# A hybrid diffusion step on one core: adaLN chunks in other places, squares ahead of the scaled copies, a fourth unnormed tile behind the pool layer

## The chip, the cores and the metric

The kernel runs on one NeuronCore of a Trainium2 chip. The metric is the device time of one launch in microseconds (us). Five engines matter: TensorE (PE, matrix products), ScalarE (ACT, copies and activation functions), VectorE (DVE, elementwise work), the SyncE queue (SP), which issues the weight transfers, and the DMA engines. GpSimd does nearly nothing here.

## The reference, cut to what matters

One inference step of a trunk of four layers with D = 1024 channels over 384 tokens: 128 context tokens and 256 latent tokens, each group with a conditioning vector of its own. All weights are float32.

```python
for i in range(DEPTH):                                # 4 layers
    kind = i % 3                                      # 0 gMLP, 1 pool, 2 attention
    sh1, sc1, gt1, sh2, sc2, gt2 = split(silu(cond) @ w_ada[i] + b_ada[i], 6)
    h = rms_norm(x, g_mix[i]) * (1 + sc1) + sh1
    y = mixer[kind](h)
    x = x + gt1 * y
    h = rms_norm(x, g_ffn[i]) * (1 + sc2) + sh2
    a, u = split(h @ w_ffn_in[i], 2)                  # 2 x 2816 columns
    x = x + gt2 * ((gelu(conv3(a)) * u) @ w_ffn_out[i])
```

The line with `w_ada` is the adaLN: for each layer six vectors of 1024 values, for two conditionings, each from a 1024 x 1024 block of weights. That is 24 blocks of eight 128 x 1024 chunks.

## The kernel before

**Activations and products.** x lies transposed in SBUF, as eight tiles d of 128 channels x 384 tokens. A float32 product is made of three passes at reduced precision: a weight is split into `whi` (a rounded copy) and `wlo` (the rest), an activation into `hh` and `hl`, and `mm3` (L688) adds hh·whi, hh·wlo and hl·whi in PSUM.

**Weights.** All weights come in one long list of chunks, in the order of a plan (`chunk_plan`), each of 128 x 1024 float32 (512 KB), through a ring of five buffers `wraw`. The SP queue issues them in order, and a buffer is given back in order. ACT makes `whi` of a chunk (L349), DVE makes `wlo` (L356), up to three chunks ahead of PE, in four buffers each.

**The phases.** For each layer the plan has the mixer's phases (`gr`, `gv`, `gu`, `go` for gMLP; `p` for the pool layer; `qkv`, `at`, `o` for attention) and then the FFN's: `fr` and `fi` (the first product, 22 tiles f of 128 columns of a and of u) and `fo` (the second). Below, go0, fo0, fi1, o2 and so on name a phase and its layer; go3 is that of the last layer. An output phase (go, o, fo) works through the output tiles d in pairs (0,1), (2,3), (4,5), and then 6 and 7 alone.

**adaLN chunks.** They stand in the same list, between the weight chunks. The table `ADA` says which of them belong to which phase, and the planner (`weave`) spreads them over the phase. An "ad" chunk is worked on DVE: two multiply-and-sum instructions of 1024 elements (L391), one for each conditioning. An "ap" chunk is worked on PE (L409). Since all engines run their own instructions in program order, an ad chunk stands on DVE between the `wlo` of its neighbours.

**Residual and what follows it.** When an output tile d is done, `residual` (L464) adds it to x on DVE, in two instructions (context and latent tokens). Then `prep.after(d)` makes what the next sub-layer needs before the norm is known: ACT writes hh = round(A·x) in two instructions (L624), DVE writes hl = A·x - hh in two (L626), ACT squares x (L477) and DVE adds the square to `acc` (L479). At the end the sum's last term is added (L484), PE sums over partitions (`cs`, L536), and from that comes the factor `rbs` of the norm. In fo0 ACT also adds the pool's bias to x (L1655). In the pool layer the residual stands at L1057. The output phase fo1, ahead of attention, makes squares only, and fo3 nothing.

**Unnormed tiles.** The first product of an FFN begins before the norm is known: its first `NR` = 3 tiles f use A·x as it stands, and the factor `rbs` is applied to the results on DVE (L714, L719). Meanwhile `norm` makes normed activations for the later tiles (L585 to L598).

**The start.** In layer 0 the first adaLN block (`a0`) is needed at once: its chunks are multiplied on PE (L1550) between the products of gMLP's first phase (L862), through a `hook` that `vmm` calls after the first of the three products of each k.

Of the kernel before, what the change touches and what calls it, by code (L numbers as in the profile page):

```python
# [99 lines left out]
def chunk_plan():  # L100
# [11 lines left out]
    for l in range(DEPTH):  # L112
# [15 lines left out]
        if kind == 0:  # L128
            phase(l, "go", out_chunks("go", j, 16))
        elif kind == 2:  # L130
            phase(l, "at", [])
            phase(l, "o", out_chunks("o", j, 8))
            n = len(plan) - len(out_chunks("o", j, 8))
            plan[n - 6:n + 2] = plan[n:n + 2] + plan[n - 6:n]
        phase(l, "fi", [("fr", l, kk, 0) for kk in range(4)] + [("fi", l, f, kk) for f in range(2, NF)
# [145 lines left out]
class Prog:  # L281
# [326 lines left out]
    def prep(self, l, which, extra=None):  # L608


        nc = self.nc
        self.ada_need(l, 3 * which + 1)
        A = self.gains(l, which)
        sh = self.prm[:, l, 24 * which:24 * which + 8, :]
        res = {"acc": self.new_acc(), "A": A}

        def after(d):
            if d == 5:
                self.ada_need(l, 3 * which)
                nc.vector.tensor_copy(self.hh[:, :, T:TE], sh)  # L620
                nc.vector.tensor_tensor(out=self.hl[:, :, T:TE], in0=sh, in1=self.hh[:, :, T:TE].bitcast(F32),
                                        op=ALU.subtract)
            for c, (t0, t1) in enumerate(GRPS):
                nc.scalar.activation(self.hh[:, d, t0:t1], self.x[:, d, t0:t1], AF.Copy, scale=A[:, d, c:c + 1])  # L624
            for c, (t0, t1) in enumerate(GRPS):
                nc.vector.scalar_tensor_tensor(out=self.hl[:, d, t0:t1], in0=self.x[:, d, t0:t1],  # L626
                                               scalar=A[:, d, c:c + 1], in1=self.hh[:, d, t0:t1].bitcast(F32),
                                               op0=ALU.mult, op1=ALU.subtract)
            res["sq"] = self.square(d, res["acc"])
            if extra is not None:  # L630
                extra(d)

        return res, after
# [56 lines left out]

    def ffn(self, l, pr, follow, stat_k):

# [5 lines left out]
        with self.tc.tile_pool(name=f"ffn{l}", bufs=1) as fp:  # L698
# [11 lines left out]
            def epi_a(f, pa, pu):  # L710
                if f >= NR:
                    return f, pa, None, pu, None
# [9 lines left out]
            def epi_b(st):  # L722
# [4 lines left out]
                for c, (t0, t1) in enumerate(GRPS):  # L727
                    p0, p1 = pos[c]
                    if f < NR:
                        nc.scalar.activation(ab[:, p0:p1], a1[:, t0:t1], AF.Identity, bias=be[:, c:c + 1])  # L730
                    else:
                        nc.scalar.activation(ab[:, p0:p1], a1[:, t0:t1], AF.Copy)
# [7 lines left out]
            def epi_c(st, t):  # L740
                f, _, _, u, bu = st
                g = self.tmp.tile([128, T], F32, tag="gg", name="gg")
                if f >= NR:
                    for c, (t0, t1) in enumerate(GRPS):
# [46 lines left out]
            for f in range(2, NF):  # L791
                w0 = TE if f < NR else T
                pa, pu = self.bank()[:, :w0], self.bank()[:, :w0]
                now, prev = (prev, []) if f == 5 else (prev[:1], prev[1:])
                for kk in range(2):
# [4 lines left out]
                    else:  # L800
                        gs = [epi_c(st, t) for st, t in zip(sts, ts)]
                        w = self.w_get("fi")
                        for st, g in zip(sts, gs):
                            self.split_act(g, gh[st[0]], gl[st[0]])
                    if f < NR:
                        norm(3)
                    for k4 in range(4):
                        k = 4 * kk + k4
                        r = (hh[:, k, :], hl[:, k, :]) if f < NR else (nh[:, k, :], nl[:, k, :])
                        self.mm3([(pa, 256 * k4), (pu, 256 * k4 + 128)], w, r, k == 0, k == 7)  # L810
# [30 lines left out]
    def gmlp(self, l, j, prep, pr=None, hook=None):  # L841
# [7 lines left out]
        with self.tc.tile_pool(name=f"gmlp{l}", bufs=1) as gp:  # L849
# [7 lines left out]
            def vmm(ps, w, cs, k):  # L857
                for p in range(3):
                    for i in range(3):
                        for n, c in enumerate(cs):  # L860
                            hs = (vl if p == 2 else vh)[:, k, 128 * i:128 * i + 128]
                            nc.tensor.matmul(ps[n][i], hs, w[p == 1][:, c:c + 512],  # L862
                                             start=(k == 0 and p == 0), stop=(k == 7 and p == 2))
                    if p == 0 and hook is not None and len(cs) == 2:
                        hook(k)

# [635 lines left out]
    def run(self):  # L1502
# [104 lines left out]

        def hook(k):
            if k + 1 < KD:
                a0_put(k + 1, a0_fin(k + 1))  # L1610
                a0_mm(k + 2)
            if k == 3:
# [9 lines left out]
        for l in range(DEPTH):  # L1622
            kind, j = l % 3, l // 3
            prep = lambda l=l: self.prep(l, 1)
            if l == 0:
                pr = self.gmlp(l, j, prep, None, hook)
            elif kind == 0:
# [31 lines left out]

            pr = self.ffn(l, pr, follow, 4 if kind == 1 else 2)  # L1660
        self.mm_ctx.close()
# [38 lines left out]
```

## Time and profile before

| what | value |
|---|---|
| median of 3 runs | 1789.51 us (1787.81 to 1791.0) |
| the profiled execution, its own time | 1788.39 us |
| span of the profiled execution | 1786.6 us |
| PE busy | 1754.6 us, 98% |
| PE's weight loads busy | 1675.2 us, 94% |
| DVE busy | 1371.8 us, 77% |
| ACT busy | 872.2 us, 49% |
| chain that ended last | PE 61%, DVE 22%, ACT 8%, DMA 4% |

How to read it: the busy share is an average over stages of different kinds. Where the time of PE's gaps goes is to be read from the rows at each gap, which name the engine and the line that ended the wait. The granted clock (PEclk) is a share of 2.4 GHz; 0.5 is the lower level, 1.2 GHz.

### The profile page before, as it was taken

What the parts mean: (1) busy time and instruction counts of PE and PEld (TensorE: products, weight loads), DVE (VectorE), ACT (ScalarE), POOL (GpSimd) and SP (SyncE); (2) the same over time, 40 slices, a digit from 0 to 9 for tenths busy, and PEclk for the clock granted to TensorE, in tenths of its full rate; (3) what the DMA queues carried; (4) which work ended last, traced back from release to release, by engine and by line L of the source; (5) the groups of instructions that cost most, each with busy time, mean ns of one, the idle gap of its engine ahead of it and who ended that gap; (6) DMA issues with size and microseconds to landing.
All of it is one profiled execution on the core that took longest, in us unless ns stands there. A gap on an engine that the chain in (4) does not pass through costs nothing.

```text
span 1786.6 us, 26835 instructions
## 1 busy us (share of the span) xinstructions
PE 1754.6 (98%) x10230; PEld 1675.2 (94%) x10230; DVE 1371.8 (77%) x2369; ACT 872.2 (49%) x1635; POOL 1.8 (0%) x30
## 2 busy tenths in 40 slices
PE   9999989999999999999998999999999999999999
PEld 7799889999998899998777999999988999999999
DVE  5888688888986888899687788887775767876632
ACT  3644236545455654432469565453454434755521
POOL 0000000000000000000000000000000000000000
PEclk9999999999999999999999999999999999999999
DMA  8764663555663355567550335655546344354341
GB/s 323 280 222 147 234 211 130 189 191 198 219 212 106 126 181 200 200 214 241 203 183 1 131 130 188 197 176 202 193 150 204 112 145 145 123 175 151 136 150 57
DMA packets 87636, 311.64 MB, mean 174 GB/s; under 512 B 10450, under 2 KB 10962, under 8 KB 87252
## 3 DMA queue, kind: packets, MB, share of 16 engines
q1 hardware_dynamic: 87220, 309.92, 50.9%
q8 instruction: 80, 1.31, 0.3%
q14 instruction: 48, 0.39, 0.1%
q10 hardware_dynamic: 288, 0.01, 0.0%
HBM read 308.06 MB, written 1.84 MB: 173 GB/s over the span
## 4 chain that ended last, share of the span: by engine, by line
PE 61%; DVE 22%; ACT 8%; issue 5%; DMA 4%; SPq 0%; DVEq 0%; ACTq 0%
PE mm L688 45%; DVE wlo L356 7%; DVE junk L391 7%; PE mm L862 6%; DMA wraw<-wts 4%; ACT whi L349 3%; DVE ct L736 3%; PE S L688 1%; PE mm L906 1%; ACT gg L745 1%; DVE gl L606 1%; PE adaT L688 1%; PE S L1138 1%; PE adaT L862 1%; PE psa L862 1%
## 5 line engine op out<-in xcount | busy, mean ns | idle before, releaser
L688 PE MATMUL mm<-hb,whi 128*128 128x384 f32 (+1 forms) x4064 | 888.7, 338 | 6.6 <-ACT whi L349 2.6
L688 PEld LDWEIGHTS mm<-hb,whi 128*128 128x128 f32 x4064 | 722.7, 189 | 11.6 <-ACT whi L349 3.3
L356 DVE TENSOR_TENSOR wlo<-wraw,whi 128x1024 fp32r<-128x1024 f32 (+2 forms) x390 | 466.3, 1201 | 213.7 <-ACT whi L349 212.4
L349 ACT ACTIVATE whi<-wraw 128x1024 fp32r<-128x1024 f32 (+2 forms) x390 | 399.3, 1034 | 270.3 <-PE mm L688 139.4
L688 PE MATMUL mm<-hb,wlo 128*128 128x384 f32 (+1 forms) x2032 | 521.4, 337 | 0.8 <-DVE wlo L356 0.8
L391 DVE SCALAR_TENSOR_TENSOR junk<-wraw,condb 128x1024 bf16<-128x1024 f32 x304 | 371.6, 1222 | 9.1 <-ACT condb L1618 2.7
L688 PEld LDWEIGHTS mm<-hb,wlo 128*128 128x128 f32 x2032 | 369.1, 189 | 1.3 <-DVE wlo L356 1.3
L745 ACT ACTIVATE gg<-ct 128x128 f32<-128x128 f32 (+1 forms) x152 | 47.0, 357 | 248.9 <-DVE ct L736 248.9
L688 PE MATMUL mm<-gh,whi 128*128 128x384 f32 x448 | 123.9, 338 | 3.2 <-ACT whi L349 3.2
L688 PE MATMUL mm<-gh,wlo 128*128 128x384 f32 x448 | 124.2, 338 | 2.4 <-DVE wlo L356 2.4
L688 PE MATMUL mm<-gl,whi 128*128 128x384 f32 x448 | 123.8, 338 | 0.0
L736 DVE SCALAR_TENSOR_TENSOR ct<-ab,par,ct 128x385 f32<-128x385 f32 x176 | 108.7, 619 | 6.4 <-ACT ct L734 2.7
L624 ACT ACTIVATE hb<-x,A 128x128 fp32r<-128x128 f32 x96 | 43.2, 457 | 103.9 <-DVE x L464 93.1
L862 PE MATMUL mm<-whi,hb 128*128 128x512 f32 x320 | 87.6, 399 | 0.0
L688 PEld LDWEIGHTS mm<-gh,whi 128*128 128x128 f32 x448 | 81.9, 189 | 4.1 <-ACT whi L349 4.1
L688 PEld LDWEIGHTS mm<-gh,wlo 128*128 128x128 f32 x448 | 82.0, 189 | 3.6 <-DVE wlo L356 3.6
L688 PEld LDWEIGHTS mm<-gl,whi 128*128 128x128 f32 x448 | 82.3, 189 | 0.0
L746 DVE TENSOR_TENSOR gg<-mm,gg 128x384 f32<-128x384 f32 x76 | 42.4, 558 | 47.4 <-ACT gg L745 46.7
L862 PEld LDWEIGHTS mm<-whi,hb 128*128 128x128 f32 x320 | 60.8, 190 | 15.6 <-ACT hb L573 0.4
L734 ACT ACTIVATE ct<-ab,par 128x385 f32<-128x385 f32 x88 | 62.7, 713 | 3.4
L464 DVE SCALAR_TENSOR_TENSOR x<-mm,prm,x 128x128 f32<-128x128 f32 x92 | 33.6, 411 | 22.9 <-PE mm L688 22.7
L862 PE MATMUL mm<-wlo,hb 128*128 128x512 f32 x160 | 47.8, 405 | 0.0
(286 smaller groups left out, 1651.8 us busy)
## 6 DMA issues: line engine op xcount, KB each, us to landing
wraw<-wts SPq DMA_DIRECT2D x562, 512.0 KB, 3.9
wraw<-wts SPq DMA_DIRECT2D x12, 256.0 KB, 2.6
wraw<-wts SPq DMA_DIRECT2D x8, 384.0 KB, 4.1
x<-x SPq DMA_DIRECT2D x4, 384.0 KB, 4.5
mx<-mix SPq DMA_DIRECT2D x1, 1280.0 KB, 7.8
y<-x SPq DMA_DIRECT2D x3, 384.0 KB, 3.1
condb<-condb SPq DMA_DIRECT2D x1, 1024.0 KB, 7.1
ws<-a_w_s SPq DMA_DIRECT2D x2, 512.0 KB, 4.3
```

What stands on the lines that cost most here:

```text
L349: nc.scalar.activation(hi[:, :n], t[:, :n], AF.Copy)
L356: nc.vector.tensor_tensor(out=lo[:, :n], in0=t[:, :n], in1=hi[:, :n].bitcast(F32), op=ALU.subtract)
L391: nc.vector.scalar_tensor_tensor(out=self.junk.bitcast(BF16), in0=w, scalar=1.0, in1=self.condb[:, c, :], op0=ALU.mult, op1=ALU.mult, accu ...
L464: nc.vector.scalar_tensor_tensor(out=x[:, d, t0:t1], in0=ps[:, t0:t1], scalar=self.prm[:, l, ty * 8 + d, c:c + 1], in1=x[:, d, t0:t1], op0 ...
L606: nc.vector.tensor_tensor(out=lo, in0=src, in1=hi.bitcast(F32), op=ALU.subtract)
L624: nc.scalar.activation(self.hh[:, d, t0:t1], self.x[:, d, t0:t1], AF.Copy, scale=A[:, d, c:c + 1])
L688: nc.tensor.matmul(o, w[:, c:c + nw], r, start=(first and p == 0), stop=(last and p == 2))
L734: nc.scalar.activation(t, ab[:, 1:T + 2], AF.Identity, scale=cw[1], bias=cb)
L736: nc.vector.scalar_tensor_tensor(out=t, in0=ab[:, i:i + T + 1], scalar=cw[i], in1=t, op0=ALU.mult, op1=ALU.add)
L745: nc.scalar.activation(g[:, t0:t1], t[:, t0 + c:t1 + c], GELU)
L746: nc.vector.tensor_tensor(out=g, in0=u, in1=g, op=ALU.mult)
L862: nc.tensor.matmul(ps[n][i], hs, w[p == 1][:, c:c + 512], start=(k == 0 and p == 0), stop=(k == 7 and p == 2))
```

## The change

Four things are changed, and no result is computed differently otherwise than by the order of roundings.

1. `prep.after(d)`: the square (ACT) and its sum (DVE) stand first. Then ACT writes A·x in two instructions into a buffer `xt`, ACT copies it to hh in one instruction, and DVE makes hl = xt - hh in one plain subtraction instead of two scaled ones.
2. The table `ADA`: ad chunks per phase, before and after: gu0 10 and 12, go0 12 and 8, fi0 18 and 18, fo0 16 and 18, fi1 18 and 20, fo1 22 and 20, fi2 16 and 18, fo2 12 and 14, gv3 8 and 8, go3 4 and 8, fi3 8 and 8. The eight chunks of block (2, 5) were ap chunks in attention, and are now ad chunks in fi2; the phase "at" and the exchange of two `o` chunks with six of them are gone.
3. The FFN behind the pool layer takes `NR` + 1 = 4 unnormed tiles.
4. At the start the hook is in two: the finished adaLN values are put to use after the first product of a k, and the next `a0` products (L1550) stand after its second product (`wlo`) instead of after the first.

```diff
--- before.py
+++ after.py
@@ -46,19 +46,18 @@
-    (0, "gu"): [("ad", 0, 2), ("ad", 0, 3, 0, 2)],
-    (0, "go"): [("ad", 0, 3, 2, 8), ("ad", 0, 5, 0, 6), ("ap", 1, 1)],
-    (0, "fi"): [("ad", 0, 5, 6, 8), ("ad", 1, 2), ("ad", 1, 0)],
-    (0, "fo"): [("ad", 1, 4), ("ad", 1, 3)],
-    (1, "fi"): [("ad", 1, 5), ("ad", 2, 1), ("ad", 2, 0, 0, 2)],
-    (1, "fo"): [("ad", 2, 0, 2, 8), ("ad", 2, 4), ("ad", 2, 3)],
+    (0, "gu"): [("ad", 0, 2), ("ad", 0, 3, 0, 4)],
+    (0, "go"): [("ad", 0, 3, 4, 8), ("ad", 0, 5, 0, 4), ("ap", 1, 1)],
+    (0, "fi"): [("ad", 0, 5, 4, 8), ("ad", 1, 2), ("ad", 1, 0, 0, 6)],
+    (0, "fo"): [("ad", 1, 0, 6, 8), ("ad", 1, 4), ("ad", 1, 3)],
+    (1, "fi"): [("ad", 1, 5), ("ad", 2, 1), ("ad", 2, 0, 0, 4)],
+    (1, "fo"): [("ad", 2, 0, 4, 8), ("ad", 2, 4), ("ad", 2, 3)],
-    (2, "at"): [("ap", 2, 5)],
-    (2, "fi"): [("ad", 3, 1), ("ad", 3, 2)],
-    (2, "fo"): [("ad", 3, 0), ("ad", 3, 4, 0, 4)],
-    (3, "gv"): [("ad", 3, 4, 4, 8), ("ad", 3, 3, 0, 4)],
-    (3, "go"): [("ad", 3, 3, 4, 8)],
+    (2, "fi"): [("ad", 2, 5), ("ad", 3, 1), ("ad", 3, 0, 0, 2)],
+    (2, "fo"): [("ad", 3, 0, 2, 8), ("ad", 3, 2)],
+    (3, "gv"): [("ad", 3, 4)],
+    (3, "go"): [("ad", 3, 3)],
@@ -128,10 +127,7 @@
-            phase(l, "at", [])
-            n = len(plan) - len(out_chunks("o", j, 8))
-            plan[n - 6:n + 2] = plan[n:n + 2] + plan[n - 6:n]
@@ -620,13 +616,13 @@
+            res["sq"] = self.square(d, res["acc"])
+            t = self.tmp.tile([128, T], F32, tag="gg", name="xt")
-                nc.scalar.activation(self.hh[:, d, t0:t1], self.x[:, d, t0:t1], AF.Copy, scale=A[:, d, c:c + 1])
-            for c, (t0, t1) in enumerate(GRPS):
-                nc.vector.scalar_tensor_tensor(out=self.hl[:, d, t0:t1], in0=self.x[:, d, t0:t1],
-                                               scalar=A[:, d, c:c + 1], in1=self.hh[:, d, t0:t1].bitcast(F32),
-                                               op0=ALU.mult, op1=ALU.subtract)
-            res["sq"] = self.square(d, res["acc"])
+                nc.scalar.activation(t[:, t0:t1], self.x[:, d, t0:t1], AF.Copy, scale=A[:, d, c:c + 1])
+            nc.scalar.activation(self.hh[:, d, 0:T], t, AF.Copy)
+            nc.vector.tensor_tensor(out=self.hl[:, d, 0:T], in0=t, in1=self.hh[:, d, 0:T].bitcast(F32),
+                                    op=ALU.subtract)
@@ -688,7 +684,7 @@
-    def ffn(self, l, pr, follow, stat_k):
+    def ffn(self, l, pr, follow, stat_k, nr):
@@ -708,7 +704,7 @@
-                if f >= NR:
+                if f >= nr:
@@ -726,7 +722,7 @@
-                    if f < NR:
+                    if f < nr:
@@ -740,7 +736,7 @@
-                if f >= NR:
+                if f >= nr:
@@ -789,7 +785,7 @@
-                w0 = TE if f < NR else T
+                w0 = TE if f < nr else T
@@ -802,11 +798,11 @@
-                    if f < NR:
+                    if f < nr:
-                        r = (hh[:, k, :], hl[:, k, :]) if f < NR else (nh[:, k, :], nl[:, k, :])
+                        r = (hh[:, k, :], hl[:, k, :]) if f < nr else (nh[:, k, :], nl[:, k, :])
@@ -861,8 +857,8 @@
-                    if p == 0 and hook is not None and len(cs) == 2:
-                        hook(k)
+                    if p < 2 and hook is not None and len(cs) == 2:
+                        hook[p](k)
@@ -1605,10 +1601,12 @@
-        def hook(k):
+        def hook0(k):
-                a0_mm(k + 2)
+
+        def hook1(k):
+            a0_mm(k + 2)
@@ -1623,7 +1621,7 @@
-                pr = self.gmlp(l, j, prep, None, hook)
+                pr = self.gmlp(l, j, prep, None, (hook0, hook1))
@@ -1657,7 +1655,7 @@
-            pr = self.ffn(l, pr, follow, 4 if kind == 1 else 2)
+            pr = self.ffn(l, pr, follow, *((4, NR + 1) if kind == 1 else (2, NR)))

```

All lines behind the table stand four lines earlier in the changed kernel up to the pool's code (L391 becomes L387, L464 L460, L1550 L1546).

PE at the start of layer 0, before. `psa` is the result of an a0 chunk, `a0T` its transposition, L862 the product of gMLP:

```order
L862 MATMUL mm<-whi,hb_83 128x512 x6
L1564 MATMUL a0T<-cst,a0row 128x2 x2
L1550 MATMUL psa<-wraw,cond 32x256 x8
L862 MATMUL mm<-wlo,hb_83 128x512 x6
L862 MATMUL mm<-whi,hb_83 128x512 x12
L1564 MATMUL a0T<-cst,a0row 128x2 x2
```

The same place after the change:

```order
L858 MATMUL mm<-whi,hb_83 128x512 x6
L1560 MATMUL a0T<-cst,a0row 128x2 x2
L858 MATMUL mm<-wlo,hb_83 128x512 x6
L1546 MATMUL psa<-wraw,cond 32x256 x8
L858 MATMUL mm<-whi,hb_83 128x512 x12
L1560 MATMUL a0T<-cst,a0row 128x2 x2
```

The eight matmuls on `wraw` moved behind the six on `wlo`.

DVE in fo0, at output tiles 2 and 3 and the chunks behind them, before (`hb` is hh and hl, `prm` the adaLN values):

```order
L464 SCALAR_TENSOR_TENSOR x<-mm,prm,x 128x128
L464 SCALAR_TENSOR_TENSOR x<-mm,prm,x 128x256
L626 SCALAR_TENSOR_TENSOR hb_84<-x,A,hb_84 128x128
L626 SCALAR_TENSOR_TENSOR hb_84<-x,A,hb_84 128x256
L479 TENSOR_TENSOR acc<-acc,sq 128x384
L464 SCALAR_TENSOR_TENSOR x<-mm,prm,x 128x128
L464 SCALAR_TENSOR_TENSOR x<-mm,prm,x 128x256
L626 SCALAR_TENSOR_TENSOR hb_84<-x,A,hb_84 128x128
L626 SCALAR_TENSOR_TENSOR hb_84<-x,A,hb_84 128x256
L479 TENSOR_TENSOR acc<-acc,sq 128x384
L356 TENSOR_TENSOR wlo<-wraw,whi 128x1024
L391 SCALAR_TENSOR_TENSOR junk,prm<-wraw,condb 128x1024 x2
```

After the change, from the ad chunk ahead of them:

```order
L387 SCALAR_TENSOR_TENSOR junk,prm<-wraw,condb 128x1024 x2
L460 SCALAR_TENSOR_TENSOR x<-mm,prm,x 128x128
L460 SCALAR_TENSOR_TENSOR x<-mm,prm,x 128x256
L475 TENSOR_TENSOR acc<-acc,sq 128x384
L624 TENSOR_TENSOR hb_84<-xt,hb_84 128x384
L460 SCALAR_TENSOR_TENSOR x<-mm,prm,x 128x128
L460 SCALAR_TENSOR_TENSOR x<-mm,prm,x 128x256
L475 TENSOR_TENSOR acc<-acc,sq 128x384
L624 TENSOR_TENSOR hb_84<-xt,hb_84 128x384
L352 TENSOR_TENSOR wlo<-wraw,whi 128x1024
L387 SCALAR_TENSOR_TENSOR junk,prm<-wraw,condb 128x1024 x2
```

The sum of squares moved ahead of hl, hl became one instruction, and one more ad chunk stands ahead of the pair.

ACT at the same two tiles of fo0, before:

```order
L624 ACTIVATE hb_84<-x,A 128x128
L624 ACTIVATE hb_84<-x,A 128x256
L477 ACTIVATE sq<-x 128x384
L1655 ACTIVATE x<-x,pgb 128x128
L1655 ACTIVATE x<-x,pgb 128x256
```

And after, for one tile d:

```order
L473 ACTIVATE sq<-x 128x384
L622 ACTIVATE xt<-x,A 128x128
L622 ACTIVATE xt<-x,A 128x256
L623 ACTIVATE hb_84<-xt 128x384
L1653 ACTIVATE x<-x,pgb 128x128
L1653 ACTIVATE x<-x,pgb 128x256
```

The square moved to the front, and one copy of 384 elements came in behind the two scaled ones.

## Rows read from the trace of the kernel before

**Rows 1.** The page, part 1: busy time (share) x instructions.

```profile
PE 1754.6 (98%) x10230; PEld 1675.2 (94%) x10230; DVE 1371.8 (77%) x2369; ACT 872.2 (49%) x1635; POOL 1.8 (0%) x30
```

**Rows 2.** Timeline of PE at its waits: start, us, instruction, [idle before <-releaser].

```profile
20.15 0.64 PE L1550 MATMUL psa<-wraw,cond 128*32 128x256 f32 x8 [1.73 <-DMA wraw<-wts]
20.72 2.33 PE L862 MATMUL mm<-wlo,hb 128*128 128x512 f32 x6
...
246.17 0.44 PE L688 MATMUL mm<-hb,whi 128*128 128x384 f32 x1 [2.58 <-ACT whi L349]
...
260.84 0.80 PE L536 MATMUL cs<-ones,acc 128*128 128x1 f32 x6 [2.09 <-DVE acc L484]
...
600.13 0.98 PE L688 MATMUL mm<-hb,whi 128*128 128x384 f32 x4 [2.26 <-DVE hb L589]
...
602.21 0.41 PE L688 MATMUL mm<-hb,whi 128*128 128x384 f32 x1 [0.23 <-DVE u L719]
```

**Rows 3.** Stretches: length, busy (x) of PE, PEld, DVE, ACT, POOL; PEclk, DMA.

```profile
246.10:253.60 7.50, 6.62 (x20) 6.36 (x21) 7.35 (x12) 0.96 (x2) 0.00 (x0) 0.54 0.45 149
443.00:534.50 91.50, 91.19 (x527) 90.87 (x526) 81.06 (x134) 42.49 (x71) 0.00 (x0) 1.00 0.62 211
1201.00:1292.40 91.40, 91.40 (x529) 91.40 (x529) 69.84 (x112) 35.61 (x53) 0.00 (x0) 1.00 0.57 193
1438.00:1506.50 68.50, 68.50 (x398) 68.50 (x398) 49.05 (x82) 28.37 (x43) 0.26 (x6) 1.00 0.48 157
```

**Rows 4.** Timeline of DVE in fo0, output tiles 2 and 3.

```profile
491.75 0.74 DVE L464 SCALAR_TENSOR_TENSOR x<-mm,prm,x 128x128 f32<-128x128 f32 x2
492.57 0.98 DVE L626 SCALAR_TENSOR_TENSOR hb<-x,A,hb 128x128 fp32r<-128x128 f32 x2
...
493.96 0.74 DVE L464 SCALAR_TENSOR_TENSOR x<-mm,prm,x 128x128 f32<-128x128 f32 x2
...
497.48 1.23 DVE L356 TENSOR_TENSOR wlo<-wraw,whi 128x1024 fp32r<-128x1024 f32 x1 [1.23 <-ACT whi L349]
...
501.03 1.22 DVE L356 TENSOR_TENSOR wlo<-wraw,whi 128x1024 fp32r<-128x1024 f32 x1
```

**Rows 5.** Timeline of ACT, the same place.

```profile
492.13 0.90 ACT L624 ACTIVATE hb<-x,A 128x128 fp32r<-128x128 f32 x2 [1.57 <-DVE x L464]
492.94 0.51 ACT L477 ACTIVATE sq<-x 128x384 f32<-128x384 f32 x1
493.48 0.81 ACT L1655 ACTIVATE x<-x,pgb 128x128 f32<-128x128 f32 x2
```

**Rows 6.** Timelines of ACT and of DVE in layer 1's norm.

```profile
581.47 0.53 ACT L588 ACTIVATE hb<-nt 128x384 fp32r<-128x384 f32 x1
```

```profile
582.03 0.56 DVE L589 TENSOR_TENSOR hb<-nt,hb 128x384 fp32r<-128x384 f32 x1 [0.95 <-ACT hb L588]
```

**Rows 7.** Timelines of DVE and of PE in fo0.

```profile
453.60 2.36 DVE L356 TENSOR_TENSOR wlo<-wraw,whi 128x1024 fp32r<-128x1024 f32 x2
...
488.20 1.23 DVE L391 SCALAR_TENSOR_TENSOR junk<-wraw,condb 128x1024 bf16<-128x1024 f32 x1 [0.43 <-DMA wraw<-wts]
```

```profile
523.05 0.45 PE L688 MATMUL mm<-gh,wlo 128*128 128x384 f32 x1 [0.31 <-DVE wlo L356]
```

**Rows 8.** Timelines of DVE and of PE at the end of o2.

```profile
1007.81 0.74 DVE L464 SCALAR_TENSOR_TENSOR x<-S,prm,x 128x128 f32<-128x128 f32 x2 [1.06 <-PE S L688]
...
1019.39 0.56 DVE L484 TENSOR_TENSOR acc<-acc,sq 128x384 f32<-128x384 f32 x1
```

```profile
1020.19 0.72 PE L536 MATMUL cs<-ones,acc 128*128 128x1 f32 x6
```

**Rows 9.** Timelines of DVE and of PE behind the pool layer.

```profile
567.32 0.56 DVE L484 TENSOR_TENSOR acc<-acc,sq 128x384 f32<-128x384 f32 x1
```

```profile
572.53 0.72 PE L536 MATMUL cs<-ones,acc 128*128 128x1 f32 x6
```

**Rows 10.** Timeline of PE in attention.

```profile
922.83 1.07 PE L409 MATMUL psa<-wraw,cond 128*32 128x256 f32 x16
```

## The prediction

> **What bounds the kernel now.** I read the page's first part for the shares, then PE's timeline for its gaps, then at each gap the timelines of DVE and ACT. PE is busy 1754.6 of 1786.6 us [rows 1], so at most 32 us can be won from its gaps, and a little more where it runs at the lower clock. The gaps that matter come from DVE or from what stands behind it. At the end of go0 PE waits 2.58 us for a `whi`, then 2.09 for the sum of squares [rows 2], and in between the granted clock is 0.54: 20 matmuls take 7.5 us [rows 3]. Behind the pool layer it waits 2.26 for a normed tile [rows 2]. At the start it waits 1.73 for a transfer, and the six products behind it then take 2.33, at the lower level [rows 2].
>
> DVE, at 77%, is not the bound on average, but in stages it is. In fo0 it works through without a pause that isn't one of its own chain: at 523.05 PE waits 0.31 for a `wlo` [rows 7], though PE is busy 91.19 of 91.50 us in the stretch [rows 3]. So DVE arrives there just in time, and whatever it is given more in fo0 comes out at PE. In fo2, with the same products and fewer ad chunks, DVE is busy 69.84 of 91.40 us [rows 3]: there more fits in.
>
> **The rearranged step of a tile d.** Before, residuals of two neighbouring tiles start 2.21 us apart (491.75 and 493.96 [rows 4]); ACT's scaled copies begin 0.38 after the residual's first half and run beside it [rows 4, 5], and hl follows at once. After, DVE does the residual (0.74), then ACT in a row the square (0.51), two scaled copies (0.90) and the new copy, for which L588 is the same instruction (0.53 [rows 6]), and only then comes hl (0.56 [rows 6]). The next residual stands behind hl in DVE's order. By durations that is 0.74 + 0.51 + 0.90 + 0.53 + 0.56 = 3.24; with starts a little ahead of ends, 3.2. So each tile holds DVE **1.0 us longer**, though DVE's own work gets shorter: 0.98 for the two scaled instructions becomes 0.56 [rows 4, 6], 0.42 less, or some 20 us of busy time over 48 tiles (6 output phases of 8). Layer 1's norm already has this shape, and there DVE stands idle 0.95 before L589, for the copy [rows 6]. Where a weight chunk follows, its `whi` is behind the new copy too: from the second residual to the `wlo` is 3.52 now (493.96 to 497.48 [rows 4]) and gets longer by the copy, 0.53, and by 0.36 because the square must await the whole residual (0.74 instead of 0.38). A pair of tiles thus blocks DVE's queue of chunks for 5.73 + 1.0 + 0.9 = 7.6 instead of 5.73: **1.9 more per pair**, with an end at 0 if ACT overlaps more than I see, and 2.3 at most.
>
> The Trainium skill (Perfetto Trace Analysis, Optimizing Scalar/DVE Operations) says that each such instruction has a fixed overhead of some 60 ns on DVE and 93 ns on ACT, and that fewer, larger ones raise the throughput of a saturated engine. By that rule the fused hl is a gain where DVE is full: in fo0 eight tiles would give back 0.42 each, 3.4 us, instead of costing. The 0.95 before L589 speaks against it here: the engine is full of waits in its own order, not of work.
>
> **Terms, phase by phase** (against the profiled execution, 1788.39).
> - Start: six `wlo` products stand ahead of the a0 chunk, so they fill the wait of 1.73 and its lower clock (2.33 for six of 512 columns; 384 columns take 91.40 / 529 = 0.173 at full clock [rows 3], so six of 512 would take 1.4 and 0.9 is lost). Gain between 1.2 and 2.9, the wait with that loss and a little more; I take **-2.5**.
> - go0: four ad chunks fewer. One costs 2.4 on DVE: from `wlo` to `wlo` with one ad chunk between is 3.55 [rows 4], less the `wlo`, 1.18 [rows 7]. That gives back 9.6; three pairs take 5.7, tile 6 1.0, tile 7 1.4 (its last sum now waits for hl: it ends 3.24 + 0.56 = 3.8 after the residual's start, before 0.38 + 0.90 + 0.51 + 0.56 = 2.35 [rows 4 to 6]). Net -1.5 if DVE's queue alone decides; if the gaps simply go, 2.58 + 2.09 + some 4 of lower clock (20 matmuls of 0.173 would take 3.5 of the 7.5 us [rows 3]), -8.7. I take **-4.5**, since the late residuals wait for PE and not for DVE.
> - fo0: two ad chunks more, 4.8, and three pairs, 5.7, on a DVE that is full; less 0.8 for gaps in which it waits for a transfer, such as 0.43 at 488.20 [rows 7]. **+9.7** (4 to 12).
> - Pool layer and its FFN: eight tiles at 1.0 more and 1.4 at the last, where the sum of squares has 4.65 to spare (567.88 to 572.53 [rows 9]). Some early tiles wait for PE anyway; I take +2.3. The fourth unnormed tile takes away the wait of 2.26 for the norm, but right behind it PE waits for a bank of an earlier unnormed tile, which DVE frees at L719 (0.23 at 602.21 [rows 2]): that wait grows into the gap, and the tile's two extra scalings are DVE work, two of 0.56, +1.1. Together **+3.4** (0 to 6). Moving two ad chunks from fo1 to fi1 gives 0: DVE is late through both.
> - Attention: 16 matmuls of an ap chunk pair take 1.07 on PE [rows 10], four pairs go. PE has gaps there for ACT, so they lie in these: **-0.7** (-3 to 0).
> - o2: the residual of tile 4 waits for PE (1.06 [rows 8]), so DVE is on time there. From it on one pair, tile 6 and tile 7 add 1.9 + 1.0 + 1.4 = 4.3: the last sum ends at 1019.95 + 4.3, and PE wants it at 1020.19 [rows 8]. A new wait, **+4.5** with the restart (2 to 6).
> - fi2 and fo2: two ad chunks more each, on a DVE with 21.6 us to spare in fo2 [rows 3]: I take **+0.6**, an estimate between 0 and 1.5, since in fi2 they come early and PE may wait once.
> - go3: four ad chunks more, 9.6, three pairs, 5.7, and the last two tiles, 2.4, together 17.7 against 19.45 to spare (68.50 - 49.05 [rows 3]), part of which lies ahead of the first of them. The last sum comes late as in o2: **+4.5** (0 to 8).
> - Lower clock behind the new waits of 4 us, as behind 2.58 in go0: **+1.0** (0 to 4).
>
> Sum: -2.5 - 4.5 + 9.7 + 3.4 - 0.7 + 4.5 + 0.6 + 4.5 + 1.0 = +16.0, so 1804.4 for an execution like the profiled one; the median lies 1.1 above that one, and I say **1805**.
>
> **The rivals.**
> A. *Faster.* The copy runs beside DVE's other work and blocks no queue: the pair costs nothing, and the busy time that DVE loses is a gain where it is full. Then fo0 is +4.8 - 3.4 = +1.4, o2 and go3 are 0, the start and go0 give 2.9 and 8.7, the pool layer's 2.26 goes: about -12, **1777**. It decides if the residual of the next tile were ahead of hl in DVE's order; the order rows say that it isn't. The Trainium skill's rule on larger instructions (Perfetto Trace Analysis, Optimizing Scalar/DVE Operations), above, would give the same sign.
> B. *Nothing to see.* The blocked queue costs half (1.0 a pair: fo0 +7, o2 and go3 +1.5 each), and go0 and the start give 10: **1790**.
> C. *Milder.* The new wait behind o2 is half as long and go3 has room: 2.2 + 4.5 less, **1798**.
> D. *Worse.* After each new wait PE falls to the lower clock, as it did after 2.58 in go0, at about 4 each, three times: **1817**.
> E. *The fourth unnormed tile does what it is for*: the 2.26 goes and no bank is waited for: 3.4 less, inside the range.
>
> **How the numbers follow.** About 0.2% (3.6 us) is what a measurement of this kernel can tell from no change. My forecast with C and D has 0.80 (0.50, 0.18, 0.12), B 0.08, A 0.12. The range leaves out A, a part of B and the far end of D: 1791 to 1817.
>
> **What would show it.** In the trace of the changed kernel: DVE idle about 0.9 before each L624, and residuals 3.2 apart; PE waiting for `wlo` or `whi` in fo0, some 10 us in all; PE waiting about 4 us for `cs` behind o2 and go3; no wait at 246; a wait for u behind the pool layer in place of that for the norm; the wait for the transfer at 20 us gone. I am wrong if residuals still start 2.2 apart, if fo0 takes as long as before, or if go0's gaps stay.

## The result, and the profile after

The changed kernel takes 1814.14 us (median of 4, 1810.43 to 1817.09), the kernel before 1789.63 beside it: ratio **1.0137**, 95% interval 1.0115 to 1.0158, some 24.5 us slower. Forecast were 1805 and +15.5, with 1791 to 1817 as the range. The sign, the cause and most terms came out; go0's gain was put too high and o2's loss too low. The profiled execution took 1810.43 us, the lowest of the four, with a span of 1808.5: 21.9 more than before in the span. The phases are compared in these two profiled executions, so some 2.5 of the 24.5 us are in no trace shown here. Three experiments below (old step, last sum first, square first) have one execution that is 17 to 21 us longer than most of their others, which lifts their ratios by 0.0005 to 0.0009 above those of the medians.

The page, part 1, after (against [rows 1]):

```profile
PE 1761.9 (97%) x10164; PEld 1678.1 (93%) x10164; DVE 1377.4 (76%) x2356; ACT 890.8 (49%) x1683; POOL 1.8 (0%) x30
```

DVE is busy for 5.6 us more: eight adaLN chunks came over from PE, and hl got cheaper (17.0 more with the table alone, 12.8 less with the new step alone, in the experiments below). So the 22 us are no work of DVE's, and of the 7.3 that PE is busy longer a good part is the lower clock, below. The rest are waits. DVE's longest ones, in order of their total (us, times, longest):

```profile
DVE wlo L352 <- ACT whi L345: 191.9, 200, 5.8
DVE gg L742 <- ACT gg L741: 47.2, 71, 0.7
DVE hb L624 <- ACT hb L623: 47.0, 48, 1.8
DVE acc L475 <- ACT sq L473: 23.1, 42, 0.7
```

The third row is the new wait: DVE stands before each of the 48 hl, 47.0 us in all. The fourth has grown from 3.6 to 23.1: the sum now stands close behind the residual, before its square is done. DVE's timeline in fo0, output tiles 2 and 3 (against [rows 4]):

```profile
495.00 0.74 DVE L460 SCALAR_TENSOR_TENSOR x<-mm,prm,x 128x128 f32<-128x128 f32 x2
496.33 0.56 DVE L475 TENSOR_TENSOR acc<-acc,sq 128x384 f32<-128x384 f32 x1 [0.59 <-ACT sq L473]
497.58 0.56 DVE L624 TENSOR_TENSOR hb<-xt,hb 128x384 fp32r<-128x384 f32 x1 [0.69 <-ACT hb L623]
498.05 0.74 DVE L460 SCALAR_TENSOR_TENSOR x<-mm,prm,x 128x128 f32<-128x128 f32 x2
...
502.27 1.23 DVE L352 TENSOR_TENSOR wlo<-wraw,whi 128x1024 fp32r<-128x1024 f32 x1 [1.08 <-ACT whi L345]
```

Residuals are 3.05 apart (2.21 before, 3.2 forecast), and from the first to the next `wlo` it is 7.27 us (5.73 before, 7.6 forecast). PE's timeline at its main waits (against [rows 2, 7, 8]):

```profile
255.06 1.41 PE L532 MATMUL cs<-ones,acc 128*128 128x1 f32 x6 [4.52 <-DVE acc L480]
...
476.33 0.62 PE L684 MATMUL mm<-gh,whi 128*128 128x384 f32 x2 [1.53 <-ACT whi L345]
477.59 0.62 PE L684 MATMUL mm<-gh,wlo 128*128 128x384 f32 x2 [0.64 <-DVE wlo L352]
...
502.29 0.62 PE L684 MATMUL mm<-gh,whi 128*128 128x384 f32 x2 [1.88 <-ACT whi L345]
503.55 0.73 PE L684 MATMUL mm<-gh,wlo 128*128 128x384 f32 x2 [0.64 <-DVE wlo L352]
...
527.65 0.44 PE L684 MATMUL mm<-gh,whi 128*128 128x384 f32 x1 [0.75 <-ACT whi L345]
528.91 0.44 PE L684 MATMUL mm<-gh,wlo 128*128 128x384 f32 x1 [0.82 <-DVE wlo L352]
...
608.35 0.44 PE L684 MATMUL mm<-hb,whi 128*128 128x384 f32 x1 [1.74 <-ACT be L713]
...
1025.39 0.95 PE L684 MATMUL mm<-hb,whi 128*128 128x386 f32 x4 [1.41 <-DVE x L460]
...
1032.92 1.38 PE L532 MATMUL cs<-ones,acc 128*128 128x1 f32 x6 [3.04 <-DVE acc L480]
...
1530.87 1.06 PE L532 MATMUL cs<-ones,acc 128*128 128x1 f32 x6 [1.93 <-DVE acc L480]
```

PE now waits for the sum of squares (`cs`) behind go0, o2 and go3, and for `whi` and `wlo` behind each pair of fo0 (6.3 us there in all). The lower clock follows behind go0 and o2 (stretches, columns as in [rows 3]):

```profile
256.30:261.40 5.10, 5.10 (x17) 5.10 (x18) 2.18 (x7) 0.20 (x1) 0.00 (x0) 0.50 0.62 206
1034.10:1039.50 5.40, 5.40 (x18) 5.40 (x19) 2.25 (x7) 0.20 (x1) 0.00 (x0) 0.50 0.55 195
```

From phase to phase (first product with `wlo` of one to that of the next, so that a phase's last wait counts to it), in us against the kernel before. The columns behind are the experiments of the next section:

| stage | forecast | after | old step | new step alone | table alone | hl later | candidate |
|---|---|---|---|---|---|---|---|
| start to the end of gr0 | -2.5 | -2.8 | -2.2 | -1.6 | +1.9 | -2.7 | -2.8 |
| gu0 | 0 | +0.8 | +0.8 | 0 | +0.8 | +0.8 | +3.2 |
| go0 and fr0 | -4.5 | -0.7 | -9.2 | +7.9 | -8.3 | -5.6 | -9.2 |
| fo0 | +9.7 | +8.9 | +5.8 | +5.2 | +4.9 | +7.8 | -0.6 |
| pool layer and its FFN (p0 to fo1) | +3.4 | +2.3 | +1.2 | +1.0 | +1.7 | +2.9 | +0.3 |
| o2 and fr2 | +4.5 | +8.2 | 0 | +6.5 | 0 | +2.8 | 0 |
| fi2 | +0.6 | +0.5 | +0.5 | 0 | +0.5 | +0.5 | +0.6 |
| go3 and fr3 | +4.5 | +5.5 | 0 | 0 | 0 | 0 | 0 |

All other stages differ by less than 0.6. The start varies by itself: with the old start the end of gr0 comes at 61.7 to 65.6 us in four traces (before, new step alone, table alone, four tiles alone), with the new one at 60.8 to 62.7 in eight.

### The profile page after: what moved, and what is told of

Its sections match the earlier page's. It is cut to its first block, busy times and chain, and to the rows that moved or that the text cites. A ratio compares the mean times of both kernels' runs of the same rounds, so it can differ in the third digit from the quotient of the medians.

```text
span 1808.5 us, 26740 instructions
## 1 busy us (share of the span) xinstructions
PE 1761.9 (97%) x10164; PEld 1678.1 (93%) x10164; DVE 1377.4 (76%) x2356; ACT 890.8 (49%) x1683; POOL 1.8 (0%) x30
## 3 DMA queue, kind: packets, MB, share of 16 engines
HBM read 308.06 MB, written 1.84 MB: 171 GB/s over the span
## 4 chain that ended last, share of the span: by engine, by line
PE 55%; DVE 25%; ACT 11%; issue 5%; DMA 3%; DVEq 0%; ACTq 0%
PE mm L684 42%; DVE wlo L352 8%; DVE junk L387 7%; PE mm L858 5%; ACT whi L345 4%; DVE ct L732 3%; DMA wraw<-wts 3%; PE mm L902 1%; ACT xt L622 1%; DVE x L460 1%; ACT gg L741 1%; DVE gl L602 1%; ACT sq L473 1%; ACT nt L583 1%; PE S L1134 1%
## 5 line engine op out<-in xcount | busy, mean ns | idle before, releaser
L387 DVE SCALAR_TENSOR_TENSOR junk<-wraw,condb 128x1024 bf16<-128x1024 f32 x320 | 390.9, 1221 | 8.5 <-ACT condb L1616 2.7
L473 ACT ACTIVATE sq<-x 128x384 f32<-128x384 f32 x49 | 25.7, 525 | 123.6 <-DVE x L460 114.8
L730 ACT ACTIVATE ct<-ab,par 128x385 f32<-128x385 f32 x88 | 62.7, 713 | 3.4
L624 DVE TENSOR_TENSOR hb<-xt,hb 128x384 fp32r<-128x384 f32 x48 | 26.8, 559 | 47.0 <-ACT hb L623 47.0
```

The source lines that it names most:

```text
L387: nc.vector.scalar_tensor_tensor(out=self.junk.bitcast(BF16), in0=w, scalar=1.0, in1=self.condb[:, c, :], op0=ALU.mult, op1=ALU.mult, accu ...
L473: nc.scalar.activation(sq, self.x[:, d, :], AF.Square)
L624: nc.vector.tensor_tensor(out=self.hl[:, d, 0:T], in0=t, in1=self.hh[:, d, 0:T].bitcast(F32), op=ALU.subtract)
L730: nc.scalar.activation(t, ab[:, 1:T + 2], AF.Identity, scale=cw[1], bias=cb)
```

## The experiments

**Theory.** The rearranged step holds DVE's queue: hl waits for ACT's longer row of instructions, and residuals, `wlo` and the last sum stand behind it. **Rival 1**: the new places of the adaLN chunks cost the time. **Rival 2**: the square's place alone, or the copy alone, does. **Rival 3**: ACT, with a copy more, is late with `whi`, and DVE's order hardly matters.

**The old step in the changed kernel.**

```
-            res["sq"] = self.square(d, res["acc"])
-            t = ...                                  # xt, the copy to hh, the plain hl
+            # the lines of the kernel before: two scaled copies, two scaled hl, the square last
```

> The changed kernel, with the step of a tile d (square, scaled copies, hl) as it was before; the table, the split hook and the fourth unnormed tile stay. Theory, that the new step holds DVE's queue: the new waits behind o2 and go3 (8.2 and 5.5 us) go, fo0 keeps only its two more adaLN chunks (about +4.3 of the 8.9), go0's gaps go (about -6), the start keeps its -2.9. Sum about -5 against the kernel before, ratio 0.997 (0.994 to 1.000). Rival, that the new places of the adaLN chunks cost the time: it stays within a third of the loss, ratio 1.009 to 1.014.

Measured: 1785.55 against 1788.44 us, ratio 0.9993 (0.9964 to 1.0022). Nearly the whole loss is gone, and so rival 1 falls. The waits behind o2 and go3 are gone, and `cs` in go0 doesn't wait either:

```profile
250.29 0.75 PE L532 MATMUL cs<-ones,acc 128*128 128x1 f32 x6
```

**The new step alone, in the kernel before.**

```
-                nc.scalar.activation(self.hh[:, d, t0:t1], self.x[:, d, t0:t1], AF.Copy, scale=A[:, d, c:c + 1])
...
+            res["sq"] = self.square(d, res["acc"])
+            t = self.tmp.tile([128, T], F32, tag="gg", name="xt")
...
```

> The kernel before, with the new step of a tile d alone. Theory of the held queue: fo0 +4.6 (three pairs at 1.54), go0 later by about 6 with its twelve chunks, pool layer and its FFN +2, o2 and its FFN +8, go3 +0 to +3; together +17 to +24, ratio 1.010 to 1.013; residuals start 3.05 apart. Rival, table at fault: within 0.3% of the kernel before.

Measured: 1808.90 us, ratio 1.0113 (1.0098 to 1.0128), so some 20 of the 24.5 us. PE's sums of waits (us, times, longest):

```profile
PE mm L688 <- ACT whi L349: 10.4, 5, 5.1
PE cs L536 <- DVE acc L484: 7.3, 2, 4.3
```

With go0's old twelve chunks that stage loses 7.9 more. In go3, with its old four, nothing: there DVE has room for the step, or for four chunks more (the old step above: 0), and not for both.

**The new table alone, in the kernel before.**

```
-    (0, "go"): [("ad", 0, 3, 2, 8), ("ad", 0, 5, 0, 6), ("ap", 1, 1)],
+    (0, "go"): [("ad", 0, 3, 4, 8), ("ad", 0, 5, 0, 4), ("ap", 1, 1)],
...
-    (2, "at"): [("ap", 2, 5)],
```

> The kernel before, with the new table (and the plan without the phase at) alone. Theory of the held queue: go0 gives back about 6, fo0 costs 4.3, gu0 0.8, fi2 0.5, fi1 and fo1 cancel, go3 and o2 cost nothing: -1.5, ratio 0.997 to 1.001. Rival, table at fault: ratio 1.008 or more.

Measured: 1786.84 us, ratio 0.9988 (0.9979 to 0.9998): a small gain. go0 gives back 8.3, fo0 takes 4.9 for its two chunks, which is the 4.8 of the forecast.

**hl behind the next residual.** The same instructions as in the changed kernel, in another order on DVE.

```
+            if res.get("hl") is not None:
+                res.pop("hl")()                      # hl of tile d - 1
             res["sq"] = self.square(d, res["acc"])
...
-            nc.vector.tensor_tensor(out=self.hl[:, d, 0:T], in0=t, ...)
+            def low(d=d, t=t): nc.vector.tensor_tensor(out=self.hl[:, d, 0:T], in0=t, ...)
+            if d < KD - 1: res["hl"] = low
+            else: low()
```

> The changed kernel, with hl of a tile written on DVE behind the next tile's residual instead of ahead of it (same instructions, only their order on DVE). Theory of the held queue: neighbouring residuals start about 1.8 to 2.3 apart instead of 3.05, and most of the loss goes, ratio 0.993 to 1.001. Rival, that ACT's extra copy (0.53 x 48) delays the rounded weights by itself: half or more of the loss stays, ratio above 1.006.

Measured: 1795.68 us, ratio 1.0038 (1.0023 to 1.0053). Some 18 of the 24.5 us are gone by a change of order alone. Residuals are now 1.80 apart. DVE's timeline at tiles 2 and 3 of fo0:

```profile
490.52 0.74 DVE L460 SCALAR_TENSOR_TENSOR x<-mm,prm,x 128x128 f32<-128x128 f32 x2
491.17 0.55 DVE L628 TENSOR_TENSOR hb<-xt,hb 128x384 fp32r<-128x384 f32 x1
...
492.32 0.74 DVE L460 SCALAR_TENSOR_TENSOR x<-mm,prm,x 128x128 f32<-128x128 f32 x2
...
497.09 1.23 DVE L352 TENSOR_TENSOR wlo<-wraw,whi 128x1024 fp32r<-128x1024 f32 x1 [2.33 <-ACT whi L345]
```

and ACT's, the last copies and the `whi` behind them:

```profile
494.90 0.53 ACT L625 ACTIVATE hb<-xt 128x384 fp32r<-128x384 f32 x1
495.33 0.79 ACT L1662 ACTIVATE x<-x,pgb 128x128 f32<-128x128 f32 x2
496.02 2.51 ACT L345 ACTIVATE whi<-wraw 128x1024 fp32r<-128x1024 f32 x3
```

Yet from the first residual to the `wlo` it is 6.57, longer than the 5.73 of before: DVE waits 2.33 for `whi`, which stands behind the copies on ACT. So rival 3 has a share: in the whole kernel DVE's order is the larger part, and what is left is ACT's row. In fo0 it is the other way round: there the order gives back 1.1 us of the 8.9 (the two chunks alone cost 4.9), while go0, o2 and go3 give back 4.9, 5.4 and 5.5. The result lies outside the expected 0.993 to 1.001, but below the rival's 1.006.

**The last sum ahead of the last hl**, on top of that order:

```
             self.nc.vector.tensor_tensor(out=pr["acc"], in0=pr["acc"], in1=pr["sq"], op=ALU.add)
+            if pr.get("last") is not None: pr.pop("last")()      # hl of tile 7
```

> The kernel with hl behind the next residual, with the last sum of squares ahead of the last hl in each output phase but fo0. If the sum's place behind hl holds PE at cs there (1.84 and 2.36 us in go0 and o2), those waits get shorter by about 1.5 each and the lower clock behind them goes: ratio 0.998 to 1.002 (1.0038 before). If it is ACT's late copies, the sum comes no earlier than the square allows and PE waits for hl(7) instead: 1.003 to 1.005.

Measured: 1792.62 us, ratio 1.0033 (1.0013 to 1.0054); the time lies in the range given for ACT's late copies, and against the run above it is not decided by the intervals. The traces speak for the sum's place: behind go0 PE waits 0.63 where it waited 1.84, behind o2 0.65 where it waited 2.36, with no wait for hl(7), and fr2's loss falls from 2.6 to 1.7. But this trace is of the shortest of the ten executions (1788.39).

```profile
250.66 0.80 PE L534 MATMUL cs<-ones,acc 128*128 128x1 f32 x6 [0.63 <-DVE acc L480]
```

**The two halves of the step, each in the changed kernel.** The copies first and the square behind them, as before, but with the new copy and the plain hl:

```
-            res["sq"] = self.square(d, res["acc"])
             t = self.tmp.tile([128, T], F32, tag="gg", name="xt")
...
+            res["sq"] = self.square(d, res["acc"])
```

> The changed kernel, with the square behind the copies as before, but with the new copy and the plain hl. The copy's half of the held queue alone: neighbouring residuals about 2.75 apart (2.21 before, 3.05 with both), a pair of fo0 about 6.8 instead of 7.27, the last sum 0.7 to 0.9 later than before instead of 1.3. Theory of the held queue: between the changed kernel and the one with the old step, ratio 1.005 to 1.010. Rival, that the square's place is what costs: ratio 0.998 to 1.002, like the old step.

Measured: 1800.89 us, ratio 1.0072 (1.0055 to 1.0089). Residuals are 2.82 apart, a pair of fo0 takes 6.88. DVE waits 1.14 for the copy, longer than L589 did in [rows 6]:

```profile
494.98 0.74 DVE L460 SCALAR_TENSOR_TENSOR x<-mm,prm,x 128x128 f32<-128x128 f32 x2
496.86 0.56 DVE L623 TENSOR_TENSOR hb<-xt,hb 128x384 fp32r<-128x384 f32 x1 [1.14 <-ACT hb L622]
...
497.80 0.74 DVE L460 SCALAR_TENSOR_TENSOR x<-mm,prm,x 128x128 f32<-128x128 f32 x2
```

The square first, but the old copies and the old hl:

```
+            res["sq"] = self.square(d, res["acc"])
             for c, (t0, t1) in enumerate(GRPS):
                 nc.scalar.activation(self.hh[:, d, t0:t1], self.x[:, d, t0:t1], AF.Copy, scale=A[:, d, c:c + 1])
...
-            res["sq"] = self.square(d, res["acc"])
```

> The changed kernel, with the square first but hl as before from x and A in two scaled instructions, without the new copy. Residuals about 2.5 apart, a pair of fo0 6.2 to 6.4. Theory of the held queue: about a third of the loss, ratio 1.002 to 1.006; rival, that the square's place costs nothing or everything: 0.998 to 1.000, or 1.010 and more.

Measured: 1794.13 us, ratio 1.0045 (1.0018 to 1.0072). Its profiled execution took 1813.70 us, with the excess in layer 1, so of its trace only the distances in layer 0 are used: residuals 2.47 apart, a pair 6.53. In order of the pair's length, with the ratio of each: old step 5.73 (in the kernel before) and 0.9993; square first 6.53 and 1.0045; hl later 6.57 and 1.0038; copies first 6.88 and 1.0072; both 7.27 and 1.0137. Rival 2 falls in both its forms: each half costs a part. For the square's half that rests on the distances more than on its time, whose interval meets that of the old step.

**The split hook alone, in the kernel before.**

```
-                    if p == 0 and hook is not None and len(cs) == 2:
-                        hook(k)
+                    if p < 2 and hook is not None and len(cs) == 2:
+                        hook[p](k)
```

> The kernel before, with the split hook at the start alone. The wait of 1.73 for a transfer and the lower clock behind it go: 2.2 to 2.9 us less up to the end of the phase gr, nothing elsewhere, ratio 0.9984 to 0.9988. Rival, that the transfer is late anyway and the wait moves behind the second product: within 0.5 us, ratio 0.9997 to 1.000.

Measured: 1787.03 against 1787.43 us, ratio 1.0002 (0.9993 to 1.0011). The start is 2.5 us shorter than in the trace before, and about 2 on the mean of the traces named above: the six `wlo` products now take 1.64 (2.33 in [rows 2]) and the transfer is there in time.

```profile
18.12 1.64 PE L862 MATMUL mm<-wlo,hb 128*128 128x512 f32 x6
19.69 1.07 PE L1550 MATMUL psa<-wraw,cond 128*32 128x256 f32 x16
...
242.08 0.44 PE L688 MATMUL mm<-hb,whi 128*128 128x384 f32 x1 [1.20 <-ACT whi L349]
...
249.50 0.97 PE L688 MATMUL mm<-hb,wlo 128*128 128x386 f32 x4 [1.17 <-DVE wlo L356]
...
256.75 1.41 PE L536 MATMUL cs<-ones,acc 128*128 128x1 f32 x6 [3.43 <-DVE acc L484]
```

But at the end of go0 PE, 2.5 us earlier, waits 3.43 for `cs` instead of 2.09, with 1.2 and 1.17 before, and then runs at the lower clock (in the kernel before, that stretch lies ahead of `cs` [rows 3]): go0 and fr0 together take 1.4 longer. Neither expectation said so. In this trace about half of the gain is given back 230 us later, and in the whole kernel's time none is left that can be measured. That an earlier start is always given back there isn't shown: in the trace of the next experiment the start is 2.0 shorter, with the old hook, and go0 and fr0 are 0.4 shorter.

**Four unnormed tiles alone, in the kernel before.**

```
-            pr = self.ffn(l, pr, follow, 4 if kind == 1 else 2)
+            pr = self.ffn(l, pr, follow, *((4, NR + 1) if kind == 1 else (2, NR)))
```

> The kernel before, with four unnormed tiles behind the pool layer alone. Theory: the wait of 2.26 for the normed tile is replaced by one for a bank of an earlier unnormed tile of about 2, and the two extra scalings on DVE show up in layer 1: 0 to +2 us, ratio 1.000 to 1.001. Rival, that the fourth tile does what it is for: 2 to 3 us less, ratio 0.9983 to 0.999.

Measured: 1790.60 against 1787.43 us, ratio 1.0012 (1.0003 to 1.0021): it costs a little. PE's wait of 2.26 for the normed tile is now one of 2.01 for ACT's `be` of an earlier unnormed tile (a copy of two columns out of the bank of a), and one of 0.30 for u, in the other bank:

```profile
598.45 0.45 PE L688 MATMUL mm<-hb,whi 128*128 128x384 f32 x1 [2.01 <-ACT be L716]
...
599.20 0.66 PE L688 MATMUL mm<-hb,whi 128*128 128x384 f32 x1 [0.30 <-DVE u L719]
```

So the wait is replaced, as expected. But of the 2.7 us that the pool layer and its FFN take longer in this trace, only 0.6 lie in fi1; 2.1 lie in fo1, some 170 us later, where PE runs at the lower clock from 766.4 to 773.2 and from 841.5 to 844.9, before only from 769.0 to 772.4. How the fourth tile would cause that is not shown.

**A candidate**: the old step, the split hook, three unnormed tiles, go0 with 8 adaLN chunks, and the four it gives up in gu0, ahead of it, so that fo0 and layer 1 keep their numbers; from attention on the new table.

```
-    (0, "gu"): [("ad", 0, 2), ("ad", 0, 3, 0, 4)],
+    (0, "gu"): [("ad", 0, 2), ("ad", 0, 3, 0, 6)],
-    (0, "go"): [("ad", 0, 3, 4, 8), ("ad", 0, 5, 0, 4), ("ap", 1, 1)],
+    (0, "go"): [("ad", 0, 3, 6, 8), ("ad", 0, 5, 0, 6), ("ap", 1, 1)],
...
```

> A candidate: the old step of a tile, the split hook, three unnormed tiles behind the pool layer as before, go0 with 8 adaLN chunks, and the four that go0 gives up in gu0 (14), so that fo0 (16), fi1 (18) and fo1 (22) stay as before; from attention on the new table. Theory: start -2.5, go0 and its FFN's start -9, gu0 +1.6 (0.8 for each two), fo0 and layer 1 as before: ratio 0.993 to 0.996. Rival, that gu0 is full as fo0 is: gu0 +5 to +10, ratio 0.998 to 1.001.

Measured: 1780.02 against 1787.63 us, ratio **0.9958** (0.9943 to 0.9973): faster than both kernels. go0 and fr0 give 9.2, the start 2.8; gu0 costs 3.2, twice what was expected for two pairs, and PE now waits there for DVE's `ct`, part of the gMLP's own work (1.7 us in all in the trace; in the kernel before not at all). `cs` behind go0 no longer waits:

```profile
252.05 0.72 PE L532 MATMUL cs<-ones,acc 128*128 128x1 f32 x6
```

## Why the prediction was right, and where it was off

**The step of a tile** was worked out from durations and came out nearly so: 3.05 for 3.2, a pair 1.54 longer for 1.9, the last sum 1.3 later for 1.4 (in o2 it ends 3.59 after its residual's start, before 2.28). DVE's busy time fell by 12.8 us with the new step alone, not by some 20. Rival A would have needed the next residual ahead of hl; the run with that order gave back 18 of the 24.5 us, which is the point it was said to decide from. Even there A's price of nothing per pair did not come: a pair took 6.57, and the kernel was slower than before.

**fo0** (+9.7, measured +8.9): right in both its terms. Two chunks alone cost 4.9 (table alone), three pairs alone 5.2 (new step alone); together a little less than the sum. PE's waits there are 6.3 us, not the some 10 forecast; behind the second pair the lower clock adds about 1.4 (12 matmuls in 3.50 us, 503.5 to 507.0).

**Start** (-2.5, measured -2.8, about -2 on the mean of the traces): right where it stands, but it was added to the total as if it stayed. In the run with the hook alone go0 and fr0 take 1.4 of it back, which the sum left out.

**go0** (-4.5 between -1.5 and -8.7; measured -0.7, just beyond the near end, or +0.1 with gu0): the step that failed is "I take -4.5, since the late residuals wait for PE and not for DVE". In the trace after, the residuals of tiles 6 and 7 stand right behind a `wlo`, with no wait for PE:

```profile
244.38 1.22 DVE L352 TENSOR_TENSOR wlo<-wraw,whi 128x1024 fp32r<-128x1024 f32 x1
245.52 0.74 DVE L460 SCALAR_TENSOR_TENSOR x<-mm,prm,x 128x128 f32<-128x128 f32 x2
...
249.04 2.36 DVE L352 TENSOR_TENSOR wlo<-wraw,whi 128x1024 fp32r<-128x1024 f32 x2 [0.39 <-ACT whi L345]
251.32 0.73 DVE L460 SCALAR_TENSOR_TENSOR x<-mm,prm,x 128x128 f32<-128x128 f32 x2
```

So the two ends of the bound were not alternatives between which the truth is shared: DVE's queue decided alone. Four chunks less are worth 8.3 to 9.2 with the old step; the new step takes 7.9 alone. The wait of 2.58 went, as forecast, and came back as 4.52 for `cs` with a lower clock behind it, 17 matmuls in 5.10 us. One sign of being wrong thus came true: go0's gaps stay (5.0 us of waits, before 5.5). gu0's two more chunks (+0.8) I had left out.

**o2** (+4.5, measured +8.2): the failed step is "the residual of tile 4 waits for PE, so DVE is on time there". Before, it waited 1.06 [rows 8]. After, the pair ahead of it (tiles 2 and 3) is longer too, and it stands without a wait behind two `wlo`:

```profile
1013.56 0.56 DVE L624 TENSOR_TENSOR hb<-xt,hb 128x384 fp32r<-128x384 f32 x1 [0.69 <-ACT hb L623]
1014.51 2.36 DVE L352 TENSOR_TENSOR wlo<-wraw,whi 128x1024 fp32r<-128x1024 f32 x2 [0.39 <-ACT whi L345]
1016.78 0.73 DVE L460 SCALAR_TENSOR_TENSOR x<-S,prm,x 128x128 f32<-128x128 f32 x2
...
1029.18 0.73 DVE L460 SCALAR_TENSOR_TENSOR x<-adaT,prm,x 128x128 f32<-128x128 f32 x2
...
1032.22 0.55 DVE L480 TENSOR_TENSOR acc<-acc,sq 128x384 f32<-128x384 f32 x1
```

So the slack that I took for sure was spent by the same change one pair earlier. PE then waits twice, 1.41 at 1025.39 for a bank that the residual of tile 6 frees, and 3.04 for `cs`, 4.45 together, which is the size that was forecast; behind them the lower clock costs 2.3 (18 matmuls in 5.40 us instead of 3.1) and 0.7 in `cs` itself (1.38 for 0.72). That makes 7.4 of the 8.2; the rest was not traced.

**go3** (+4.5, measured +5.5), **fi2 and fo2** (+0.6, measured +0.5): right within 1 us. **Attention** (-0.7, measured -0.5 in qkv) can't be told from nothing: with the same table, old step and hl later have +0.4 and +0.5 there. **Pool layer and its FFN** (+3.4, measured +2.3): near, but by luck in its parts. The tiles cost 1.0 (new step alone) where I had 2.3, and the chunks moved from fo1 to fi1 cost 1.7 (table alone) where I had 0; alone, the parts add up to more than they cost together. For the fourth tile the wait was replaced as I said, though by ACT's `be` (L713) more than by DVE's u.

**Lower clock** (+1.0): right in kind, too small. There are five such stretches where there were three, and the three behind `cs` are in the rows of go0, o2 and go3 above. That is rival D in kind, at 1 to 3 us a stretch instead of about 4; with 1814 the time lies nearer to its 1817 than to 1805.

**The rule on fused instructions** (the Trainium skill, Perfetto Trace Analysis, Optimizing Scalar/DVE Operations) was given as a reason for the other sign. hl did become cheaper, 0.56 for 0.98. The page limits it to an engine that is saturated; DVE here was full of its own order of waits, and the cheaper instruction came with a wait of 0.98 on average before it (47.0 over 48).

What the executions leave open: the parts alone add to 1.0113, 0.9988, 1.0002 and 1.0012, in all 1.0115, against 1.0137 (1.0115 to 1.0158) for the whole. That the rest is the meeting of table and step in go3 (0 with either, 5.5 with both) fits in size, but was not run by itself. That ACT had to wait for a free buffer `xt`, which shares its buffers with others, is not seen: in the trace after, no instruction that writes it (L622) has idle time ahead of it.

## What to carry to other kernels

Where an engine works in program order, the price of an instruction is what stands behind it until its inputs are there, not its duration: before a step is made cheaper, write out its chain across engines, and let the next independent instruction go ahead of the one that waits. A gain in front of a place that another engine decides may be given back there, as in one trace here: don't add it to the sum before that place has been worked out with it. And when a change lengthens every unit of a loop, don't take the slack seen at the last unit as given: the unit ahead of it has used it.

## What the runs showed that I had not expected

The lower clock doesn't follow from a wait's size alone. In the kernel before, PE waits 2.26 us for the normed tile [rows 2] and runs at the full clock behind it, but in fo1, behind waits of 1.07 and 0.64, it runs at 0.5 (12 matmuls in 3.40 us):

```profile
767.49 0.62 PE L688 MATMUL mm<-gh,whi 128*128 128x384 f32 x2 [1.07 <-ACT whi L349]
768.75 0.83 PE L688 MATMUL mm<-gh,wlo 128*128 128x384 f32 x2 [0.64 <-DVE wlo L356]
```

```profile
600.10:603.60 3.50, 3.24 (x17) 2.95 (x18) 3.20 (x6) 2.73 (x7) 0.00 (x0) 1.00 0.30 116
769.00:772.40 3.40, 3.40 (x12) 3.40 (x12) 3.37 (x6) 1.41 (x3) 0.00 (x0) 0.50 0.56 177
```

Columns as in [rows 3]. Even the same waits, 1.56 and 0.82 us later in fo1, have the full clock behind them there, and the lower one in the run with four unnormed tiles alone (1.54 and 0.81). In the stretches counted here the lower clock cost PE 1.3 to 2.3 us (12 matmuls in 3.40 us, 18 in 5.40, by the 0.173 of the full clock), and that is what I would set for a new wait of 2 us and more, with 0 as the other end.
